# Two transformer-style blocks on one core: a sixth tile in the plain form at the head of each feed-forward network, and operand buffers moved modulo 256 bytes

## The chip, the cores and the metric

The kernel runs on one core of one Trainium2 chip. The metric is the device time of one execution in microseconds, and the time of a kernel is the median of several runs. Engines are named as in the profile: PE is TensorE (PEld is its weight load), DVE is VectorE, ACT is ScalarE, POOL is GpSimd, SP is the engine that issues the DMAs.

## The reference

An input of 512 tokens with 1024 features passes through two layers of a first block and one layer of a second block. A layer of the first block is `x += 0.5*ffn1(x)`, then a mixer of four attention variants, then `x += 0.5*ffn2(x)`, then a norm. The second block has other mixers and no feed-forward network. The change concerns the feed-forward networks alone, of which there are four (two in each layer):

```
def swiglu(h, w_gate, w_up, w_down):
    return (jax.nn.silu(h @ w_gate) * (h @ w_up)) @ w_down
```

with `h = rms_norm(x)`, 1024 features in and out, and 2816 hidden features (22 tiles of 128). All data are float32.

## The kernel before, in words

**Arithmetic.** Every float32 product is made of three matmuls in the reduced type float32r: an operand is split into a high part (an ACT copy that rounds) and a low part (a DVE subtraction), and `mm3` (line 97) adds high*high, high*low and low*high in PSUM. Tokens lie along the free dimension, so the moving operand of a matmul is an activation and the stationary operand, loaded by PEld, is a weight tile of 128x128.

**One network** (`ffn`, line 339). The 22 hidden tiles are computed one after the other by `up`, in chunks (0, 4, 8, 12, 16, 19, 22). When a chunk is done, its eight `down` steps (one for each 128 output features) are interleaved with the hidden tiles of the next chunk, two after each of them. A `down` over a chunk of four takes 12 matmuls of 512 columns, and all `down` steps of a network together take 528.

**Two forms of a hidden tile.** The first five tiles (`DIRECT = 5`) have the plain form, `direct` (line 227): for gate and up each 8 input tiles times 3 matmuls of 512 columns, 48 in all, on `xh`, `xl`, which are x times the norm's gain, split. The other 17 have a Winograd form of Strassen's product, `winograd` (line 304): gate and up are the rows of a 2x2 block product, token halves its columns, and seven products of 4 input tiles times 3 matmuls of 256 columns take the place of eight, 84 in all. Its moving operands `fh0..3`, `fl0..3` hold seven combinations of blocks of the normed input. They are made once for each network by `forms` (line 244), emitted after the first tile: per `k` two DVE scalings into temporaries `a`, `b`, four DVE subtractions into `tw`, three ACT copies into `fh` and three DVE subtractions into `fl`. `a`, `b` use the buffers `gh7`, `gl7` and `gh4`, `gl4` by turns. The weights need combinations as well, which `blocks` (line 268) makes for each tile: four sums or differences `s1` to `s4` (two on POOL, two on DVE, line 291), then seven splits (lines 298 and 299).

**Buffers of weights.** Plain tiles and `down` steps load their weights into `raw` (two buffers of 4 KB per partition in turn), and split them into `whi`, `wlo` (three buffers each). Winograd tiles load theirs into buffers of `xh`, `xl`, which are free once the plain tiles are done, but the first Winograd tile (`f == DIRECT`) loads its two halves into the two `raw` buffers (line 278) and puts `s1` to `s4` into `gh5`, `gh6`, `gl5`, `gl6`.

**Order.** A planner orders each engine's instructions by a simulated timeline; weight loads and their splits are pulled ahead by a priority offset. Each engine, and the DMA issue on SP, then runs its list in order.

**Places in SBUF.** In the compiled program of before the buffers `xh`, `xl`, `raw`, `whi`, `wlo` begin at 96 modulo 256 bytes per partition. The network's own pool (`R`, `s`, `cu`, `g..`, `f..`, `tw`) begins at 128 modulo 256, and all of its buffers are multiples of 256 bytes long. The list `PAD` (line 393) puts 0, 8, 16 and 24 floats ahead of them in the four networks. The distance from `whi`/`wlo` to `gh`, `gl`, `fh`, `fl` modulo 256 is thus 32, 64, 96 and 128 bytes in networks one to four; the distance from `whi` to `xh` is 0 in all.

**Between layers** `post_norm` (line 203) leaves a `late` function that scales the eight `x` tiles by the norm; network three (the first of layer two) calls it once after `forms` (line 381), the second block once (line 1748).

Of the kernel before, what the change touches and what calls it, by code (L numbers as in the profile page):

```python
# [12 lines left out]
F32 = mybir.dt.float32  # L13
F32R = mybir.dt.float32r
AF = mybir.ActivationFunctionType
ALU = mybir.AluOpType
# [3 lines left out]
P = 128  # L20
S = 512
D = 1024
KT = D // P
# [8 lines left out]
class Builder:  # L32
    def __init__(self, ctx, tc, A):
        self.ctx, self.tc, self.nc, self.A = ctx, tc, tc.nc, A
        self.n = 0
        self.lo_eng = tc.nc.vector
        self.late = lambda: None
        nc = self.nc
        pool = lambda name, **kw: ctx.enter_context(tc.tile_pool(name=name, bufs=1, **kw))
        self.const = pool("const")  # L40
        self.xp = pool("xp")
        self.wp = pool("wp")
        self.sm = pool("sm")
        self.ps = pool("ps", space=PSUM)
        self.ones = self.const.tile([P, P], F32, name="ones")
        nc.vector.memset(self.ones, 1.0)
        self.neghalf = self.const.tile([P, 32], F32, name="neghalf")
        nc.vector.memset(self.neghalf, -0.5)
# [154 lines left out]
    def post_norm(self, gain, bank=("t", 3)):  # L203

        nc = self.nc
        r1 = self.rstd(self.tok_sum(self.sq, bank), D)
        s2 = self.tok_sum(self.sq2, bank)
        ms = self.t(self.sm, "ms", (P, 4))
        nc.vector.tensor_tensor(out=ms, in0=s2, in1=r1, op=ALU.mult)
        nc.vector.tensor_tensor(out=ms, in0=ms, in1=r1, op=ALU.mult)  # L210
        nc.vector.tensor_scalar(out=ms, in0=ms, scalar1=1.0 / D, scalar2=EPS, op0=ALU.mult, op1=ALU.add)
        r2 = self.rsqrt(ms, (P, 4))
        r = self.t(self.sm, "r12", (P, 4))
        nc.vector.tensor_tensor(out=r, in0=r1, in1=r2, op=ALU.mult)

        def late():
            self.late = lambda: None
            R1 = self.bcast(r1, self.sm, "sqt", bank)
            for k in range(KT):
                nc.vector.scalar_tensor_tensor(out=self.x[k], in0=self.x[k], scalar=gain[:, k:k + 1], in1=R1,  # L220
                                               op0=ALU.mult, op1=ALU.mult)

        self.late = late
        return r
# [19 lines left out]
    def forms(self, gp, gain, R):  # L244


        nc = self.nc
        out = []
        lo, hi = slice(0, 256), slice(256, 512)
        flat = lambda t: t.rearrange("p e c -> p (e c)")  # L250
        sub = lambda o, x, y: nc.vector.tensor_tensor(out=o, in0=x, in1=y, op=ALU.subtract)  # L251
        for k in range(4):
            H, L = self.t(gp, f"fh{k}", (P, 7, 256), F32R), self.t(gp, f"fl{k}", (P, 7, 256), F32R)
            a, b = (self.t(gp, f"g{e}{7 - 3 * (k % 2)}") for e in "hl")
            for j, o in ((k, a), (k + 4, b)):
                nc.vector.scalar_tensor_tensor(out=o, in0=self.x[j], scalar=gain[:, j:j + 1], in1=R, op0=ALU.mult, op1=ALU.mult)
            W = self.t(gp, "tw", (P, 4, 256))
            sub(W[:, 0], a[:, hi], a[:, lo])
            sub(W[:, 1], b[:, hi], W[:, 0])
            sub(W[:, 2], b[:, hi], a[:, hi])  # L260
            sub(W[:, 3], b[:, lo], W[:, 1])
            for j, n, src in ((0, 1, a[:, lo]), (1, 2, b), (3, 4, flat(W))):
                nc.scalar.activation(out=flat(H[:, j:j + n]), in_=src, func=AF.Copy)  # L263
                sub(flat(L[:, j:j + n]), src, flat(H[:, j:j + n]).bitcast(F32))
            out.append((H, L))
        return out

    def blocks(self, gp, wgu, f):


        nc = self.nc
        with self.tc.high_priority(offset=self.ahead):
            A = []
            if f == DIRECT:
                slot = iter([(gp, f"g{t}{i}") for t in "hl" for i in (5, 6)])
                for which in range(2):
                    t = self.wp.tile([P, 1024], F32, tag="raw", name=self.name("raw"), bufs=2)
                    nc.sync.dma_start(out=t, in_=wgu[f, which])
                    A += [t[:, 0:S], t[:, S:]]
            else:  # L280
                slot = iter([(self.xp, f"x{t}{4 * (f % 2) + i}") for t in "hl" for i in range(4)])
                for which in range(2):
                    for e in range(2):
                        t = self.t(*next(slot))
                        nc.sync.dma_start(out=t, in_=wgu[f, which][:, e * S:(e + 1) * S])
                        A.append(t)
            a11, a12, a21, a22 = A
            s1, s2, s3, s4 = (self.t(*next(slot)) for _ in range(4))
            for eng, o, x, y, op in ((nc.gpsimd, s1, a21, a22, ALU.add), (nc.vector, s2, s1, a11, ALU.subtract),
                                     (nc.gpsimd, s3, a11, a21, ALU.subtract), (nc.vector, s4, a12, s2, ALU.subtract)):  # L290
                eng.tensor_tensor(out=o, in0=x, in1=y, op=op)  # L291
            out = []
            for pair in ((a11, s2), (s1, s3), (a12, s4), (a22,)):
                hi = self.wp.tile([P, 1024], F32R, tag="whi", name=self.name("whi"), bufs=3)
                lo = self.wp.tile([P, 1024], F32R, tag="wlo", name=self.name("wlo"), bufs=3)
                for e, src in enumerate(pair):
                    c = slice(e * S, (e + 1) * S)
                    nc.scalar.activation(out=hi[:, c], in_=src, func=AF.Copy)  # L298
                    nc.vector.tensor_tensor(out=lo[:, c], in0=src, in1=hi[:, c].bitcast(F32), op=ALU.subtract)  # L299
                    v = lambda t: t[:, c].rearrange("p (k m) -> p k m", k=4)  # L300
                    out.append((v(hi), v(lo)))
        return out

    def winograd(self, gp, wgu, f, F):

        nc = self.nc
        a11, s2, s1, s3, a12, s4, a22 = self.blocks(gp, wgu, f)
        pa, pb = self.bank("s", 3), self.bank("t", 3)
        lo, hi = slice(0, 256), slice(256, 512)

# [28 lines left out]
    def ffn(self, r, wgu, wd, gain, done, reorder=False):  # L339

        nc = self.nc
        with self.tc.tile_pool(name=self.name("ffn"), bufs=1, reuse_waits="tile") as gp:
            pad = next(PAD)
            if pad:
                gp.tile([P, pad], F32, name=self.name("pad"))
            R = self.bcast(r, gp, "R", ACC)
            F = None

            def up(f, i):

                u, s = self.direct(gp, wgu, f, R) if f < DIRECT else self.winograd(gp, wgu, f, F)
                nc.vector.tensor_tensor(out=u, in0=u, in1=s, op=ALU.mult)
                h = self.t(gp, f"gh{i}", dt=F32R)
                l = self.t(gp, f"gl{i}", dt=F32R)
                nc.scalar.activation(out=h, in_=u, func=AF.Copy)
                nc.vector.tensor_tensor(out=l, in0=u, in1=h.bitcast(F32), op=ALU.subtract)
                return h, l

            def down(k, f0, f1, g):

                ps = self.bank("acc", 2)
                wh, wl = self.weights(wd[k][:, f0 * P:f1 * P], (f1 - f0, P))
                for j, (h, l) in enumerate(g):
                    self.mm3(ps, wh[:, j], wl[:, j], h, l, j == 0, j == f1 - f0 - 1)
                x = self.x[k]
                if reorder and f1 == NFF:
                    t = self.t(gp, "R" if k % 2 else "xa")
                    v = lambda a: a.rearrange("p (c r) -> p r c", r=8)
                    nc.vector.scalar_tensor_tensor(out=t.rearrange("p (r c) -> p r c", r=8), in0=v(ps), scalar=0.5, in1=v(x), op0=ALU.mult, op1=ALU.add)
                    nc.scalar.activation(out=x, in_=t, func=AF.Copy)  # L370
                else:
                    nc.vector.scalar_tensor_tensor(out=x, in0=ps, scalar=0.5, in1=x, op0=ALU.mult, op1=ALU.add)  # L372

            downs = []
            for n, (f0, f1) in enumerate(zip(CHUNKS, CHUNKS[1:])):
                g = []
                for f in range(f0, f1):
                    g.append(up(f, 4 * (n % 2) + f - f0))
                    if F is None:
                        F = self.forms(gp, gain, R)  # L380
                        self.late()
                    for _ in range(-(-len(downs) // (f1 - f))):
                        downs.pop(0)()
                downs = [lambda k=k, f0=f0, f1=f1, g=g: down(k, f0, f1, g) for k in range(KT)]
# [4 lines left out]


CHUNKS = (0, 4, 8, 12, 16, 19, NFF)
DIRECT = 5
PAD = iter((0, 8, 16, 24))

POOL = 'ac'
COMB = (0, 1, 2)
# [703 lines left out]
class Mixer2(Mixer1):  # L1100
# [609 lines left out]
    def output(self, part, scratch, out=None):  # L1710
# [32 lines left out]
        if part == "x":  # L1743
            self.acc = [[self.t("oacc") for _ in range(2)] for _ in range(4)]
            for k in range(KT):
                b.x[k] = b.t(b.xp, f"x{k}")
                nc.sync.dma_start(out=b.x[k], in_=scratch[k])
            b.late()
            return
        if part != "last":  # L1750
            return first(int(part))
# [259 lines left out]
```

## Time and profile before

| what | value |
|---|---|
| median of 3 runs | 2564.03 us (2547.78 to 2564.64) |
| the profiled execution | 2554.28 us, its span 2552.4 us |
| mean granted clock of PE in it | 0.979 |
| busy PE / PEld | 2437.3 us (95%) / 2108.9 us (83%) |
| busy DVE / ACT / POOL | 1832.3 us (72%) / 1270.1 us (50%) / 718.4 us (28%) |
| read from HBM | 209.14 MB, 85 GB/s over the span |

The four networks' Winograd parts begin at 74.46, 765.17, 1124.95 and 1825.40 us of the span. Matmuls are pipelined, so a matmul's own duration in the profile (0.28 or 0.39 us) overlaps its neighbours', and the cost of one is the distance from its start to the next one's. In a table of stretches, "(x1660)" is the number of instructions that ran in the stretch, and PEclk the granted clock as a share of full speed.

### The profile page before, as it was taken

To read this page: it belongs to the slowest core of one execution; us is meant where nothing else is said; L and a number is where in the kernel's file an instruction comes from. 1 tells how busy PE (TensorE), PEld (TensorE's weight loads), DVE (VectorE), ACT (ScalarE), POOL (GpSimd) and SP (SyncE) were. 2 spreads that over 40 slices of the span, in tenths; PEclk is the share of its full clock that TensorE was granted. 3 is DMA by queue.
4 is the path that set the end of the run, shared out by engine and by line. 5 is a ranking of instruction groups with operands and counts; after the bars stand their busy time and mean duration, and the time that the engine had idled before them with its cause. 6 is when DMAs were issued, how large, how long until landed. Compare 5 with 4: busy or idle time off the path is not lost. (4 is left out here: it accounts for less than half of the span.)

```text
span 2552.4 us, 39475 instructions
## 1 busy us (share of the span) xinstructions
PE 2437.3 (95%) x14904; PEld 2108.9 (83%) x14904; DVE 1832.3 (72%) x3275; ACT 1270.1 (50%) x2422; POOL 718.4 (28%) x567
## 2 busy tenths in 40 slices
PE   8899999999999999989999999999999999899998
PEld 6899988886688999879999888767799997777867
DVE  7777776976577777797777689755877767755543
ACT  5344456676534444534444576764344445334553
POOL 1211115652212111311110447223111104452322
PEclk9899999999999999989999999999999999999999
DMA  4333233211233332323332432012333314220111
GB/s 147 110 103 106 89 119 100 90 46 37 66 107 96 105 105 73 94 92 97 103 99 67 134 102 81 20 53 75 112 100 104 104 59 148 62 76 32 41 46 56
DMA packets 113824, 220.53 MB, mean 86 GB/s; under 512 B 22160, under 2 KB 33489, under 8 KB 113633
## 3 DMA queue, kind: packets, MB, share of 16 engines
q1 hardware_dynamic: 110224, 217.67, 28.1%
q8 instruction: 117, 1.92, 0.3%
q10 hardware_dynamic: 3408, 0.33, 0.1%
q14 instruction: 75, 0.61, 0.1%
HBM read 209.14 MB, written 8.78 MB: 85 GB/s over the span
## 5 line engine op out<-in xcount | busy, mean ns | idle before, releaser
L88 ACT ACTIVATE whi<-raw 128x1024 fp32r<-128x1024 f32 (+4 forms) x343 | 263.1, 769 | 480.1 <-PE t L316 208.8
L291 POOL TENSOR_TENSOR xl<-xh,xh 128x512 f32<-128x512 f32 x128 | 190.1, 1488 | 859.9 <-DVE wlo L299 436.8
L316 PE MATMUL t<-fh,wlo 128*128 128x256 f32 x1088 | 308.5, 284 | 2.1 <-DVE wlo L299 2.1
L316 PE MATMUL t<-fh,whi 128*128 128x256 f32 x1088 | 308.0, 283 | 1.5 <-ACT fh L263 0.8
L316 PE MATMUL t<-fl,whi 128*128 128x256 f32 x1088 | 307.6, 283 | 0.0
L99 PE MATMUL acc<-gh,whi 128*128 128x512 f32 x704 | 278.1, 396 | 8.0 <-DVE x L372 4.6
L100 PE MATMUL acc<-gl,whi 128*128 128x512 f32 x704 | 279.0, 397 | 0.0
L101 PE MATMUL acc<-gh,wlo 128*128 128x512 f32 x704 | 277.3, 394 | 0.5 <-DVE wlo L89 0.5
L89 DVE TENSOR_TENSOR wlo<-raw,whi 128x512 fp32r<-128x512 f32 (+3 forms) x269 | 220.3, 819 | 51.0 <-ACT whi L88 50.1
L316 PE MATMUL s<-fh,whi 128*128 128x256 f32 x816 | 231.5, 284 | 11.3 <-ACT whi L298 6.0
L316 PE MATMUL s<-fh,wlo 128*128 128x256 f32 x816 | 231.7, 284 | 9.3 <-DVE wlo L299 9.3
L316 PE MATMUL s<-fl,whi 128*128 128x256 f32 x816 | 230.8, 283 | 1.1 <-DVE fl L251 1.1
L89 POOL TENSOR_TENSOR wlo<-raw,whi 128x1024 fp32r<-128x1024 f32 (+2 forms) x74 | 167.1, 2260 | 220.7 <-ACT whi L88 207.2
L316 PEld LDWEIGHTS t<-fh,whi 128*128 128x128 f32 x1088 | 207.5, 191 | 8.2 <-ACT whi L298 1.1
L316 PEld LDWEIGHTS t<-fl,whi 128*128 128x128 f32 x1088 | 208.0, 191 | 6.2
L316 PEld LDWEIGHTS t<-fh,wlo 128*128 128x128 f32 x1088 | 208.2, 191 | 3.0 <-DVE wlo L299 3.0
L298 ACT ACTIVATE whi<-xh 128x512 fp32r<-128x512 f32 x192 | 121.5, 633 | 178.9 <-issue 95.7
L299 DVE TENSOR_TENSOR wlo<-xh,whi 128x512 fp32r<-128x512 f32 x192 | 160.0, 833 | 33.4 <-ACT whi L298 33.0
L372 DVE SCALAR_TENSOR_TENSOR x<-acc,x 128x512 f32<-128x512 f32 x184 | 126.5, 687 | 76.1 <-PE acc L101 75.9
L298 ACT ACTIVATE whi<-xl 128x512 fp32r<-128x512 f32 x256 | 152.8, 621 | 50.1 <-PE t L316 43.5
L299 DVE TENSOR_TENSOR wlo<-xl,whi 128x512 fp32r<-128x512 f32 x256 | 169.7, 683 | 0.0
L316 PEld LDWEIGHTS s<-fh,whi 128*128 128x128 f32 x816 | 155.2, 190 | 15.6 <-ACT whi L298 6.4
(714 smaller groups left out, 6529.7 us busy)
## 6 DMA issues: line engine op xcount, KB each, us to landing
xh<-in_ffn_gu_dram SPq DMA_DIRECT2D x256, 256.0 KB, 2.6
raw<-in_ffn_d_dram SPq DMA_DIRECT2D x128, 256.0 KB, 2.7
raw<-in_ffn_gu_dram SPq DMA_DIRECT2D x48, 512.0 KB, 3.6
raw<-in_w2f_dram SPq DMA_DIRECT2D x25, 512.0 KB, 3.6
raw<-in_ffn_d_dram SPq DMA_DIRECT2D x64, 192.0 KB, 2.4
xs<-x SPq DMA_DIRECT2D x24, 256.0 KB, 4.0
raw<-in_a_dram SPq DMA_DIRECT2D x12, 512.0 KB, 3.5
x<-xs SPq DMA_DIRECT2D x24, 256.0 KB, 3.0
```

Of the source, the lines that this page charges most:

```text
L88: nc.scalar.activation(out=hi, in_=raw, func=AF.Copy)
L89: (lo_eng or self.lo_eng).tensor_tensor(out=lo, in0=raw, in1=hi.bitcast(F32), op=ALU.subtract)
L99: mm(out=out, lhsT=lh, rhs=rh, start=start, stop=False)
L100: mm(out=out, lhsT=lh, rhs=rl, start=False, stop=False)
L101: mm(out=out, lhsT=ll, rhs=rh, start=False, stop=stop)
L291: eng.tensor_tensor(out=o, in0=x, in1=y, op=op)
L298: nc.scalar.activation(out=hi[:, c], in_=src, func=AF.Copy)
L299: nc.vector.tensor_tensor(out=lo[:, c], in0=src, in1=hi[:, c].bitcast(F32), op=ALU.subtract)
L316: nc.tensor.matmul(out=out, lhsT=x[:, k], rhs=y[:, j], start=start and k == 0 and n == 0, stop=stop and k == 3 and n == 2, skip_group_chec ...
L372: nc.vector.scalar_tensor_tensor(out=x, in0=ps, scalar=0.5, in1=x, op0=ALU.mult, op1=ALU.add)
```

## The change

The diff, without the lines that only pass on an argument:

```diff
 def late():                       # in post_norm
-    self.late = lambda: None
+    self.late = lambda: lambda k: None
     R1 = self.bcast(r1, self.sm, "sqt", bank)
-    for k in range(KT):
-        nc.vector.scalar_tensor_tensor(out=self.x[k], in0=self.x[k], scalar=gain[:, k:k + 1], in1=R1,
-                                       op0=ALU.mult, op1=ALU.mult)
+    return lambda k: nc.vector.scalar_tensor_tensor(out=self.x[k], in0=self.x[k], scalar=gain[:, k:k + 1], in1=R1,
+                                                    op0=ALU.mult, op1=ALU.mult)
...
 for k in range(4):                # in forms
-    H, L = self.t(gp, f"fh{k}", (P, 7, 256), F32R), self.t(gp, f"fl{k}", (P, 7, 256), F32R)
-    a, b = (self.t(gp, f"g{e}{7 - 3 * (k % 2)}") for e in "hl")
+    H, L = (self.t(gp, f"f{e}{k}", (P, 1856), F32R)[:, 48:1840].rearrange("p (e c) -> p e c", e=7) for e in "hl")
+    a, b = (self.t(gp, f"g{e}5") for e in "hl")
...
+def quarters(self, wgu, f, slot):
+    out = []
+    for which in range(2):
+        for e in range(2):
+            t = self.t(*next(slot))
+            self.nc.sync.dma_start(out=t, in_=wgu[f, which][:, e * S:(e + 1) * S])
+            out.append(t)
+    return out
+
+def prefetch(self, gp, wgu):
+    return self.quarters(wgu, DIRECT, iter([(gp, f"g{t}{i}") for t in "hl" for i in (6, 7)]))
...
 if f == DIRECT:                   # in blocks
-    slot = iter([(gp, f"g{t}{i}") for t in "hl" for i in (5, 6)])
-    for which in range(2):
-        t = self.wp.tile([P, 1024], F32, tag="raw", name=self.name("raw"), bufs=2)
-        nc.sync.dma_start(out=t, in_=wgu[f, which])
-        A += [t[:, 0:S], t[:, S:]]
+    A = raw
+    t = [self.wp.tile([P, 1024], F32, tag="raw", name=self.name("raw"), bufs=2) for _ in range(2)]
+    s1, s2, s3, s4 = (x[:, e * S:(e + 1) * S] for x in t for e in range(2))
...
-    pad = next(PAD)               # in ffn
-    if pad:
-        gp.tile([P, pad], F32, name=self.name("pad"))
+    gp.tile([P, 56], F32, name=self.name("pad"))
+    raw = None
...
 def down(k, f0, f1, g):
+    if f0 == 0:
+        late(k)
...
-    t = self.t(gp, "R" if k % 2 else "xa")
+    t = self.t(gp, "cu")
...
     F = self.forms(gp, gain, R)
-    self.late()
+    late = self.late()
+    raw = self.prefetch(gp, wgu)
...
-DIRECT = 5
-PAD = iter((0, 8, 16, 24))
+DIRECT = 6
```

So each network computes six plain and 16 Winograd tiles. The first Winograd tile's weights are loaded in four quarters into `gh6`, `gh7`, `gl6`, `gl7`, emitted right after `forms`, and `s1` to `s4` lie in the two `raw` buffers. The temporaries of `forms` are one pair, `gh5`, `gl5`. The scaling of `x[k]` in network three goes with the first `down` of that `k`. The pool's buffers are moved by 56 floats (224 bytes) in all four networks, which puts `gh`, `gl` at 96 modulo 256, the same as `whi`, `wlo` (distance 0); `fh`, `fl` lie 48 floats further, at a distance of 192 bytes.

## Rows read from the trace of the kernel before

**Rows 1.** The page: busy time of PE and the others.
```profile
PE 2437.3 (95%) x14904; PEld 2108.9 (83%) x14904; DVE 1832.3 (72%) x3275; ACT 1270.1 (50%) x2422; POOL 718.4 (28%) x567
```
**Rows 2.** Stretches of 240 us inside networks 1 to 4: all PE (busy, count, clock, DMA).
```profile
100.00:340.00 240.00, 240.00 (x1660) 1.00 0.32 95
790.00:1030.00 240.00, 239.37 (x1676) 1.00 0.32 94
1160.00:1400.00 240.00, 240.00 (x1634) 1.00 0.32 94
1850.00:2090.00 240.00, 240.00 (x1649) 1.00 0.32 94
```
**Rows 3.** The same stretches: line 316 alone, PE then PEld.
```profile
100.00:340.00 240.00, 154.79 (x1262) 154.11 (x1263) 1.00 0.32 95
790.00:1030.00 240.00, 157.15 (x1286) 156.17 (x1285) 1.00 0.32 94
1160.00:1400.00 240.00, 156.14 (x1244) 155.04 (x1243) 1.00 0.32 94
1850.00:2090.00 240.00, 156.20 (x1259) 155.13 (x1258) 1.00 0.32 94
```
**Rows 4.** Timeline of PE, network 1: 40 plain matmuls, then 24 of `down`, first and last.
```profile
59.79 0.39 PE L101 MATMUL s<-xh,wlo 128*128 128x512 f32 x1
...
68.63 0.39 PE L101 MATMUL t<-xh,wlo 128*128 128x512 f32 x1
68.86 0.40 PE L99 MATMUL acc<-gh,whi 128*128 128x512 f32 x1
...
74.23 0.40 PE L101 MATMUL acc<-gh,wlo 128*128 128x512 f32 x1
```
**Rows 5.** Timeline of PE, network 2: 24 matmuls of `down`, first and last.
```profile
759.66 0.40 PE L99 MATMUL acc<-gh,whi 128*128 128x512 f32 x1
...
764.94 0.39 PE L101 MATMUL acc<-gh,wlo 128*128 128x512 f32 x1
```
**Rows 6.** The 30 us after the first Winograd matmul, networks 1 to 4: all PE.
```profile
74.46:104.46 30.00, 23.62 (x134) 0.77 0.20 61
765.17:795.17 30.00, 25.13 (x171) 0.94 0.27 81
1124.95:1154.95 30.00, 20.28 (x99) 0.72 0.19 55
1825.40:1855.40 30.00, 25.60 (x168) 0.89 0.27 78
```
**Rows 7.** The same stretches: line 316 alone, PE then PEld.
```profile
74.46:104.46 30.00, 18.51 (x109) 17.16 (x109) 0.77 0.20 61
765.17:795.17 30.00, 19.65 (x144) 18.69 (x144) 0.94 0.27 81
1124.95:1154.95 30.00, 14.99 (x74) 13.26 (x74) 0.72 0.19 55
1825.40:1855.40 30.00, 20.32 (x143) 19.70 (x143) 0.89 0.27 78
```
**Rows 8.** Timeline, network 1: a load of SP, and the POOL sum that waited for it.
```profile
68.12 0.38 SPq L278 DMA_DIRECT2D raw<-in_ffn_gu_dram  x1
...
74.48 1.59 POOL L291 TENSOR_TENSOR gh<-raw 128x512 f32<-128x512 f32 x1 [2.00 <-DMA raw<-in_ffn_gu_dram]
```
**Rows 9.** Timeline of PE: the longest waits of networks 2 and 3 in those stretches.
```profile
770.31 0.38 PE L316 MATMUL s<-fh,wlo 128*128 128x256 f32 x1 [3.09 <-DVE wlo L299]
...
1131.03 0.58 PE L316 MATMUL s<-fh,whi 128*128 128x256 f32 x1 [4.25 <-ACT whi L298]
```
**Rows 10.** Line 220, the 16 scalings of `x`: duration ns min/median/max, first and last start.
```profile
L220 DVE SCALAR_TENSOR_TENSOR x<-x,fin_g,sqt x16: 734/743/749, 1092.3 to 2468.1; 128x512 f32<-128x512 f32 x16
```
**Rows 11.** DMA issues: a quarter of a Winograd tile's weights, KB and us to landing.
```profile
xh<-in_ffn_gu_dram SPq DMA_DIRECT2D x256, 256.0 KB, 2.6
```
**Rows 12.** Line 263, the ACT copies of `forms`: idle before them until (us, times).
```profile
  DVE gh L256: 11.7, 6
```

More of the change, by code (lines that the diff above doesn't have):

```diff
@@ L216, in late @@
         def late():
-            self.late = lambda: None
+            self.late = lambda: lambda k: None
             R1 = self.bcast(r1, self.sm, "sqt", bank)
-            for k in range(KT):
-                nc.vector.scalar_tensor_tensor(out=self.x[k], in0=self.x[k], scalar=gain[:, k:k + 1], in1=R1,
-                                               op0=ALU.mult, op1=ALU.mult)
+            return lambda k: nc.vector.scalar_tensor_tensor(out=self.x[k], in0=self.x[k], scalar=gain[:, k:k + 1], in1=R1,
+                                                            op0=ALU.mult, op1=ALU.mult)
         self.late = late
@@ L266, in forms, with blocks @@
         return out
-    def blocks(self, gp, wgu, f):
+    def quarters(self, wgu, f, slot):
[8 more added lines that the diff above has]
+        return self.quarters(wgu, DIRECT, iter([(gp, f"g{t}{i}") for t in "hl" for i in (6, 7)]))
+    def blocks(self, wgu, f, raw):
         nc = self.nc
         with self.tc.high_priority(offset=self.ahead):
-            A = []
             if f == DIRECT:
-                slot = iter([(gp, f"g{t}{i}") for t in "hl" for i in (5, 6)])
-                for which in range(2):
-                    t = self.wp.tile([P, 1024], F32, tag="raw", name=self.name("raw"), bufs=2)
-                    nc.sync.dma_start(out=t, in_=wgu[f, which])
-                    A += [t[:, 0:S], t[:, S:]]
+                A = raw
+                t = [self.wp.tile([P, 1024], F32, tag="raw", name=self.name("raw"), bufs=2) for _ in range(2)]
+                s1, s2, s3, s4 = (x[:, e * S:(e + 1) * S] for x in t for e in range(2))
             else:
                 slot = iter([(self.xp, f"x{t}{4 * (f % 2) + i}") for t in "hl" for i in range(4)])
[L282 to L286, printed above, removed]
+                A = self.quarters(wgu, f, slot)
+                s1, s2, s3, s4 = (self.t(*next(slot)) for _ in range(4))
             a11, a12, a21, a22 = A
-            s1, s2, s3, s4 = (self.t(*next(slot)) for _ in range(4))
             for eng, o, x, y, op in ((nc.gpsimd, s1, a21, a22, ALU.add), (nc.vector, s2, s1, a11, ALU.subtract),
@@ L302, in blocks, with winograd @@
         return out
-    def winograd(self, gp, wgu, f, F):
+    def winograd(self, gp, wgu, f, F, raw):
         nc = self.nc
-        a11, s2, s1, s3, a12, s4, a22 = self.blocks(gp, wgu, f)
+        a11, s2, s1, s3, a12, s4, a22 = self.blocks(wgu, f, raw)
         pa, pb = self.bank("s", 3), self.bank("t", 3)
@@ L349, in up @@
             def up(f, i):
-                u, s = self.direct(gp, wgu, f, R) if f < DIRECT else self.winograd(gp, wgu, f, F)
+                u, s = self.direct(gp, wgu, f, R) if f < DIRECT else self.winograd(gp, wgu, f, F, raw)
                 nc.vector.tensor_tensor(out=u, in0=u, in1=s, op=ALU.mult)
@@ L1747, in output @@
                 nc.sync.dma_start(out=b.x[k], in_=scratch[k])
-            b.late()
+            late = b.late()
+            for k in range(KT):
+                late(k)
             return
```

## The prediction

> **What bounds the kernel now.** The page's first table comes first: PE is busy 95% of the span [rows 1], so time can only be won where PE waits, where its matmuls run slower than they could, or where there are fewer of them. The chain of waits, followed back from the end, gets lost in the second block and says nothing of the networks, so I went on to stretches of PE.
>
> Inside a network, past its head, PE never waits: 240.0 of 240 us busy in three networks, 239.37 in the second, at a granted clock of 1.00 [rows 2]. Yet the networks don't run alike. In equal time the second starts 1286 Winograd matmuls and the third 1244 [rows 3], with about the same number of `down` matmuls (total less Winograd: 398, 390, 390, 390 [rows 2, 3]). The only thing in the code that differs between them there is the pad.
>
> From the timelines come the spacings. Plain tiles, at distance 0: (68.63 - 59.79)/39 = 226.7 ns for a matmul of 512 columns [rows 4]. `Down` at distance 32, network one: (74.23 - 68.86)/23 = 233.5 ns [rows 4]. `Down` at distance 64, network two: (764.94 - 759.66)/23 = 229.6 ns [rows 5]. Networks three and four I cost as network one. The Winograd spacing is what is left of the busy time: (240.0 - 398 x 0.2335)/1262 = 116.5 ns in the first, (239.37 - 390 x 0.2296)/1286 = 116.5, (240.0 - 390 x 0.2335)/1244 = 119.7 and, likewise over 1259, 118.3 ns in the second to fourth [rows 2 to 5].
>
> At each network's head PE does wait. In the 30 us after the first Winograd matmul it starts 134, 171, 99 and 168 matmuls [rows 6], of which 109, 144, 74 and 143 are Winograd's [rows 7] and the other 25, 27, 25, 25 are of 512 columns. At the spacings above this is 18.5, 23.0, 14.7 and 22.8 us of work, so 11.5, 7.0, 15.3 and 7.2 us are lost, 41.0 in all. Part is idle time (30 - 23.62 = 6.4 us in network one), part the clock, granted at 0.72 to 0.94 there [rows 6].
>
> Why it waits can be followed in network one. The second half of the first Winograd tile's weights must have a `raw` buffer that the `down` weights hold before; its load is issued at 68.12 us, and the POOL sum that needs it starts at 74.48 [rows 8], when PE has already begun the tile at 74.46. The splits come later still, and PE waits for them: the longest waits of networks two and three are 3.09 us for a `wlo` and 4.25 us for a `whi` [rows 9].
>
> **The change part by part.**
>
> *Prefetch and own slots, sixth plain tile.* The four quarters no longer need `raw`, and between `forms` and the first Winograd tile stands one more plain tile: 48 x 0.2267 = 10.9 us of PE work [rows 4], in which POOL and DVE can make sums and splits and finish `forms`. That is longer than what is lost in networks one, two and four. I take a rest of 2.5 us for each network (one wait shorter than the 3.09 of [rows 9], and some time at the lower clock), 10 in all: **-31.0 us**. Bounds: nothing left, -41.0; network two's loss left in each of them, 41.0 - 4 x 7.0 = 13 won. What is late next, if anything, is the last of the four `forms`.
>
> The prefetch adds no bytes, but its four DMAs go through SP at the head, past the loads of plain tiles. A quarter takes 2.6 us to land [rows 11]. I cost it at nothing: the queue has a whole head of five plain tiles, over 50 us, to fit 10.4 us in. Without that cover it is up to 4 x 2.6 us for each network. `s1` to `s4` in `raw` hold back the weights of the next two `down` steps; these are needed after the tile's 84 x 0.1165 = 9.8 us, and a load of that size plus a split fits in that. Before, the raw weights held the same two buffers, until a later split. Nothing.
>
> *One Winograd tile less, one plain more.* 4 x 10.88 - 84 x (0.1165 + 0.1165 + 0.1197 + 0.1183) = 43.5 - 39.6 = **+4.0 us**, on the bound engine.
>
> *`gh`, `gl` at distance 0.* `Down` has the pattern of the plain tiles (512 columns, activation moving, weights stationary), which run at 226.7 ns at this distance [rows 4]. I take that: 528 x (3 x 6.8 + 2.9) ns = **-12.3 us** [rows 4, 5]. Bounds: this, and nothing won.
>
> *`fh`, `fl` at distance 192.* No row has it. The nearest by distance modulo 256 is 64 bytes on the other side of 0, network two with 116.5 ns; I take it, for want of a row that says more: 16 tiles x 84 x (0 + 0 + 3.2 + 1.8) ns = **-6.7 us**. Bounds: half of the plain spacing, 113.4 ns, gives -23.4; the worst network's 119.7 gives +10.5.
>
> A rule speaks against both placement terms. The Trainium skill ("TensorE: Matmul & The Clock Gate", Step-by-step: what each phase is for) says that weight load and moving operand have independent read ports, so that a load takes no bandwidth from the running matmul; by it, the place of one buffer against the other would not matter. The trace does not bear this out as far as the pads are the cause: the same matmul is spaced by 226.7, 229.6 and 233.5 ns at one clock.
>
> *Moved `late`, one pair `gh5`, `gl5`, `cu` for `xa`.* In network three eight scalings of 0.743 us [rows 10], 5.9 us of DVE, leave the head and go to the first `down` steps; DVE is busy 72% [rows 1], and the update of `x` that follows them holds up nobody for tens of us. Already in the stall's bounds; nothing more. With one pair, the scaling for the next `k` waits until ACT and DVE have read the last. DVE has its other work ahead of and between them, so I take nothing; the bound is a rival below. `cu` has two buffers, as `R` and `xa` together had: nothing.
>
> *Sum.* -31.0 - 12.3 - 6.7 + 4.0 = -46.0 us. Against the profiled execution's own 2554.3 us that is **2508 us**. The median of the runs shown lies 9.7 us above that execution; I keep to the execution.
>
> **The rivals.**
>
> *Placement does nothing.* The networks would differ for another reason, and only the head counts: -31 + 4 = -27, 2527 us. The rule of the Trainium skill on independent ports would give this time. Against it: the order of spacings follows the pads, and plain tiles in every network have one. Chance 0.08.
>
> *The head still waits.* The raw weights were only the last of several late things, and each network goes on losing 7.0 us: 2508 + 18 = 2526 us. For it: DVE is behind in the head, and one pair for `forms` takes freedom from the planner. Against it: 11 us more time. Chance 0.12.
>
> *The prefetch gets in the way.* Its 10.4 us of loads stand ahead of plain tiles' weights on SP, and PE waits for these instead: 4 x 10.4 = 42 us, 2550 us, no change. Against it: plain weights carry the higher priority. Chance 0.08.
>
> *Slower: the one pair of `forms`.* Three times in a network the scaling for the next `k` stands at the front of DVE's queue until the last copy is done, and behind it stand the low parts that PE needs in the plain tiles. ACT has waited 11.7 us in 6 times, 2.0 us each, at this place with two pairs [rows 12]. If each of the 12 waits costs PE as much as the longest one of [rows 9], 4.25 us, and the clock multiplies it as in network three (15.3 lost for 30 - 20.28 = 9.7 idle, 1.58), it is 12 x 4.25 x 1.58 = 81 us: 2508 + 81 = 2589 us. It turns the result to slower by 1% from 71/12 = 5.9 us lost for each wait. Against it: DVE's list is ordered with the waits known, and other work can stand ahead. Chance 0.06.
>
> **How the numbers follow.** The forecast has the rest, 0.66. The range adds up the bounds of the terms: -41.0 - 12.3 - 23.4 + 4.0 = -72.7, 2482 us; and -13 - 12.3 + 10.5 + 4.0 = -10.8, 2544 us. It holds the first two rivals; outside are the last two with 0.14 and some tails. One per cent is about what a measurement of this kernel can tell from no change. Faster by more than that needs under 2529 us on the execution's scale: nearly all of the forecast (0.62) and some over half of the first two rivals (0.12), 0.74. Slower: 0.06. Within 1%: 0.20.
>
> **What would show it.** After the change the 30 us behind the first Winograd matmul should hold some 200 matmuls or more at a clock near 1.00, and no wait over 3 us. `Down` should be spaced by 227 ns in all four networks, Winograd by one value in all four; the value is the least certain term. The plain tiles should stay free of waits; a wait there for `whi` names the prefetch, one for `wlo` names DVE's queue. I am wrong if the spacings of the four networks come out equal but at 120 ns, or if the head loses as much as before.

## The result and the profile after

| | before | after |
|---|---|---|
| median | 2556.01 us (4 runs, 2547.78 to 2564.64) | 2526.26 us (4 runs, 2519.19 to 2529.18) |
| the profiled execution | 2554.28 us | 2524.95 us |

The ratio of the changed kernel's runs to those of the kernel before is 0.9879, with a 95% interval of 0.983 to 0.9929: some 30 us faster, where 46 were forecast. The time lies inside the stated range.

The first lines of the page of the changed kernel:
```profile
span 2522.8 us, 39081 instructions
...
PE 2426.8 (96%) x14760; PEld 2102.4 (83%) x14760; DVE 1802.7 (71%) x3235; ACT 1259.5 (50%) x2394; POOL 706.3 (28%) x559
```
PE stays the bound [rows 1].

**The heads.** The 30 us after the first Winograd matmul of each network, all PE first (busy, count, clock, DMA), then the Winograd line alone, which is line 323 now:
```profile
90.45:120.45 30.00, 27.71 (x198) 1.00 0.32 89
772.14:802.14 30.00, 28.09 (x201) 1.00 0.32 92
1127.77:1157.77 30.00, 27.03 (x187) 0.94 0.28 84
1813.02:1843.02 30.00, 26.75 (x186) 0.94 0.30 88
```
```profile
90.45:120.45 30.00, 19.89 (x159) 19.40 (x159) 1.00 0.32 89
772.14:802.14 30.00, 20.26 (x162) 19.77 (x162) 1.00 0.32 92
1127.77:1157.77 30.00, 19.92 (x156) 19.22 (x155) 0.94 0.28 84
1813.02:1843.02 30.00, 20.80 (x156) 20.17 (x155) 0.94 0.30 88
```
Against 134, 171, 99 and 168 matmuls [rows 6, 7] there are now 198, 201, 187 and 186, and the clock is granted at 0.94 to 1.00 where it was 0.72 to 0.94. Worked out as in the prediction, with 117.8 and 226.8 ns, the heads lose 2.4, 2.1, 4.6 and 4.8 us: 13.9 in place of 41.0.

What is left is mostly one kind of wait, here in the timeline of PE of the changed kernel (start, duration, then in brackets the idle time before and what ended it):
```profile
98.75 0.39 PE L323 MATMUL s<-fh,whi 128*128 128x256 f32 x1 [1.75 <-DVE wu L326]
...
780.05 0.39 PE L323 MATMUL s<-fh,whi 128*128 128x256 f32 x1 [1.77 <-DVE wu L326]
...
1136.61 0.39 PE L323 MATMUL s<-fh,whi 128*128 128x256 f32 x1 [2.97 <-DVE wu L326]
...
1822.28 0.39 PE L323 MATMUL s<-fh,whi 128*128 128x256 f32 x1 [1.77 <-DVE wu L326]
```
The weights are no longer late [rows 9]: in network one the first POOL sum on them starts 13.6 us before the first Winograd matmul at 90.45 us, where it started with it before [rows 8].
```profile
76.88 2.20 POOL L298 TENSOR_TENSOR raw<-gl,gl 128x512 f32<-128x512 f32 x1 [45.99 <-DVE wlo L89]
```
PE waits for `wu`, the DVE sum that must have read the first product before PE may add `a12` to its bank. The timelines of ACT and DVE in network one show the copy that is the other input of `wu`, and `wu` itself:
```profile
93.90 0.36 ACT L331 ACTIVATE w<-s 128x256 f32<-128x256 f32 x1
...
98.28 0.41 DVE L326 TENSOR_TENSOR wu<-s,w 128x256 f32<-128x256 f32 x1
```
The input is there at 94.26 us. DVE, which is never idle in between, first works off splits of this tile, two sums for the next one and an update of `x`. The waits for `wu` are 8.3 of the 13.9 us; two waits for a `wlo`, of 0.5 and 1.5 us in networks one and four, and the lower clock in networks three and four are nearly all the rest.

**The spacings.** A stretch of 240 us inside networks one and three of the changed kernel, all PE and then line 323:
```profile
100.00:340.00 240.00, 240.00 (x1671) 1.00 0.31 92
...
1145.00:1385.00 240.00, 240.00 (x1670) 1.00 0.32 92
```
```profile
100.00:340.00 240.00, 156.93 (x1272) 156.03 (x1271) 1.00 0.31 92
...
1145.00:1385.00 240.00, 157.27 (x1272) 156.29 (x1272) 1.00 0.32 92
```
The two networks run alike now, 1272 Winograd matmuls each, where network one had 1262 and network three 1244 [rows 3]; that is still fewer than the 1286 that network two had. `Down`, 24 matmuls in network one of the changed kernel, first and last:
```profile
85.01 0.39 PE L99 MATMUL acc<-gh,whi 128*128 128x512 f32 x1
...
90.23 0.39 PE L101 MATMUL acc<-gh,wlo 128*128 128x512 f32 x1
```
(90.23 - 85.01)/23 = 227.0 ns, where it was 233.5 [rows 4] and 229.6 [rows 5].

The table gives, for every kernel, what was read in this way from its profile: the mean spacing of starts past the head, in ns, networks one to four; the loss in the four heads; the sum of the four networks (first matmul to last `down` of each); and block two, the time from the last network to the end, whose code no kernel changes.

| kernel | Winograd, ns | `down`, ns | heads, us | networks, us | block two, us |
|---|---|---|---|---|---|
| before | 116.9 116.6 119.9 118.5 | 233.2 228.9 233.7 233.5 | 40.8 | 1462.6 | 427.6 |
| after | 117.8 in all | 226.7 to 227.0 | 13.9 | 1426.0 | 434.5 |
| e1_place | 117.7 in all | 226.8 to 226.9 | 41.9 | 1451.2 | 426.0 |
| e2_head | 116.9 116.2 119.9 118.5 | 233.1 229.0 233.5 233.5 | 11.7 | 1433.7 | 424.7 |
| e3_six | 117.7 in all | 226.8 to 226.9 | 32.9 | 1446.4 | 427.4 |
| e4_pre5 | 117.7 to 117.8 | 226.7 to 226.9 | 34.5 | 1446.5 | 426.2 |
| e5_fsweep1 | 119.6 117.4 118.7 118.3 | 229.4 229.7 228.2 229.3 | 12.1 | 1434.4 | 426.8 |
| e6_fsweep2 | 118.3 119.7 118.7 118.5 | 233.8 232.7 232.8 229.3 | 12.6 | 1441.8 | 437.2 |
| e7_late | 117.8 in all | 226.8 to 227.1 | 12.3 | 1425.1 | 425.0 |
| e8_all64 | 114.5 116.7 116.7 116.7 | 229.7 229.0 229.0 229.1 | 12.2 | 1423.3 | 426.4 |
| e9_prio5 | 117.7 to 117.8 | 226.7 to 226.9 | 32.6 | 1444.8 | 426.1 |
| e10_prio6 | 117.8 in all | 226.7 to 227.1 | 12.0 | 1425.5 | 426.4 |
| e11_prio5b | 117.7 to 117.8 | 226.7 to 227.0 | 34.0 | 1444.8 | 435.7 |
| e12_mixed | 114.5 116.7 114.5 114.5 | 229.7 229.0 229.7 229.7 | 13.4 | 1417.6 | 422.2 |

### The profile page after: what moved, and what is told of

Read it like the earlier page. It is cut to its first block, busy times and chain, and to the rows that moved or that the text cites. A ratio compares the mean times of both kernels' runs of the same rounds, so it can differ in the third digit from the quotient of the medians.

```text
span 2522.8 us, 39081 instructions
## 1 busy us (share of the span) xinstructions
PE 2426.8 (96%) x14760; PEld 2102.4 (83%) x14760; DVE 1802.7 (71%) x3235; ACT 1259.5 (50%) x2394; POOL 706.3 (28%) x559
## 5 line engine op out<-in xcount | busy, mean ns | idle before, releaser
L298 POOL TENSOR_TENSOR xl<-xh,xh 128x512 f32<-128x512 f32 x120 | 175.2, 1461 | 722.2 <-DVE wlo L306 402.5
L323 PE MATMUL t<-fh,wlo 128*128 128x256 f32 x1024 | 288.8, 282 | 2.2 <-DVE wlo L306 2.0
L323 PE MATMUL t<-fh,whi 128*128 128x256 f32 x1024 | 288.6, 282 | 0.0
L323 PE MATMUL t<-fl,whi 128*128 128x256 f32 x1024 | 288.5, 282 | 0.0
L323 PE MATMUL s<-fh,whi 128*128 128x256 f32 x768 | 216.8, 282 | 8.3 <-DVE wu L326 8.3
L323 PE MATMUL s<-fh,wlo 128*128 128x256 f32 x768 | 216.5, 282 | 0.0
L323 PEld LDWEIGHTS t<-fl,whi 128*128 128x128 f32 x1024 | 192.9, 188 | 5.1
L380 DVE SCALAR_TENSOR_TENSOR x<-acc,x 128x512 f32<-128x512 f32 x184 | 126.4, 687 | 66.4 <-PE acc L101 66.0
L442 PE MATMUL acc<-whi,xh 128*128 128x256 f32 (+1 forms) x576 | 166.3, 292 | 1.9 <-DVE gate L1140 1.3
L442 PE MATMUL acc<-wlo,xh 128*128 128x256 f32 (+1 forms) x576 | 167.2, 291 | 0.4 <-DVE wlo L89 0.4
L442 PE MATMUL acc<-whi,xl 128*128 128x256 f32 (+1 forms) x576 | 166.7, 291 | 0.0
```

Source lines behind the costliest of these rows:

```text
L323: nc.tensor.matmul(out=out, lhsT=x[:, k], rhs=y[:, j], start=start and k == 0 and n == 0, stop=stop and k == 3 and n == 2, skip_group_chec ...
L442: mm = lambda l, r, st=False, sp=False: nc.tensor.matmul(out=ps[i], lhsT=l, rhs=r, start=st, stop=sp, skip_group_check=True)
```

## The experiments

My theory going in: the heads and the placement each give a part of the gain, and both can be had alone. The rivals: that placement does nothing; and, for the heads, that either the sixth plain tile or the own slots alone would do.

**e1_place: the placement alone**, on the kernel before.
```diff
-    H, L = self.t(gp, f"fh{k}", (P, 7, 256), F32R), self.t(gp, f"fl{k}", (P, 7, 256), F32R)
+    H, L = (self.t(gp, f"f{e}{k}", (P, 1856), F32R)[:, 48:1840].rearrange("p (e c) -> p e c", e=7) for e in "hl")
-    pad = next(PAD)
-    if pad:
-        gp.tile([P, pad], F32, name=self.name("pad"))
+    gp.tile([P, 56], F32, name=self.name("pad"))
-    t = self.t(gp, "R" if k % 2 else "xa")
+    t = self.t(gp, "cu")
```
Expected: 

> The placement alone: the kernel before with the pad of 56 floats in all networks and fh, fl at their offset of 48 floats; five plain tiles, raw weights and forms as before. Theory (heads and placement each give a part): down is spaced by 227 ns and Winograd by 117 to 118 ns in all four networks, some 14 us less than before in the four networks together (about 0.995 of the time), and the 30 us after the first Winograd matmul still lose 41 us in sum. Rival (placement does nothing, the spacings come from the order of the work): spacings as before, 230 to 234 ns and 116 to 120 ns by network, and no gain.

Measured: 2543.2 us, ratio 0.9971 (0.9954 to 0.9987). `Down` is at 226.8, Winograd at 117.7 ns in all four networks, these take 11.4 us less, and the heads still lose 41.9. The waits of PE in network three's head (who waited for whom, us in total, times, longest) are as before:
```profile
PE s L316 <- ACT whi L298: 4.2, 1, 4.2
PE s L316 <- ACT fh L263: 2.5, 1, 2.5
```
So buffers moved by a few dozen bytes, with no other edit that PE sees, change the spacing. The rival that placement does nothing is out.

**e2_head: the head alone**, on the changed kernel.
```diff
-    H, L = (self.t(gp, f"f{e}{k}", (P, 1856), F32R)[:, 48:1840].rearrange("p (e c) -> p e c", e=7) for e in "hl")
+    H, L = self.t(gp, f"fh{k}", (P, 7, 256), F32R), self.t(gp, f"fl{k}", (P, 7, 256), F32R)
-    gp.tile([P, 56], F32, name=self.name("pad"))
+    pad = next(PAD)                       # PAD = iter((0, 8, 16, 24))
+    if pad:
+        gp.tile([P, pad], F32, name=self.name("pad"))
```
Expected: 

> The head alone: six plain tiles, own slots, one pair for forms, late by k, with pads of 0, 8, 16 and 24 floats and no offset of fh, fl, as before. Theory: the heads lose about 15 us in all instead of 41, one plain tile more costs 4 us for four networks, so some 22 us less than before (0.991); the spacings are the ones of before, network by network (233, 230, 233, 233 ns for down). Rival (placement does nothing): the whole gain of the changed kernel, 30 us (0.988), and equal spacings in the four networks.

Measured: 2528.59 us, ratio 0.9899 (0.986 to 0.9938). Heads lose 11.7 us, the spacings are those of before to within 0.4 ns, and the networks take 28.9 us less. With e1's 11.4 that is 40.3 against 36.6 for both: the parts add up, less a few us. The ratio alone could not tell the two answers apart (the rival's 0.988 is inside the interval); the spacings do.

**e3_six: six plain tiles without own slots.**
```diff
-    A = raw
-    t = [self.wp.tile([P, 1024], F32, tag="raw", name=self.name("raw"), bufs=2) for _ in range(2)]
-    s1, s2, s3, s4 = (x[:, e * S:(e + 1) * S] for x in t for e in range(2))
+    slot = iter([(raw, f"g{t}{i}") for t in "hl" for i in (6, 7)])       # raw is gp
+    A = []
+    for which in range(2):
+        t = self.wp.tile([P, 1024], F32, tag="raw", name=self.name("raw"), bufs=2)
+        nc.sync.dma_start(out=t, in_=wgu[f, which])
+        A += [t[:, 0:S], t[:, S:]]
+    s1, s2, s3, s4 = (self.t(*next(slot)) for _ in range(4))
```
Expected: 

> The changed kernel with six plain tiles but without own slots: the first Winograd tile's weights go through the two raw buffers again, s1 to s4 into gh6, gh7, gl6, gl7. Theory (the late load of the second half is what PE waited for): the wait comes back one tile later, the heads lose 25 us or more in all, 10 us or more slower than the changed kernel. Rival (the time of one more plain tile, in which forms and DVE catch up, is what healed the heads): the heads lose about 15 us as in the changed kernel, and the time is the same.

Measured: 2535.67 us, ratio 0.9926 (0.9897 to 0.9954); the heads lose 32.9 us, networks 20.4 us more than in the changed kernel. The timelines of SP, POOL and PE of this kernel, network one (its first Winograd matmul is at 89.60 us):
```profile
80.72 0.36 SPq L292 DMA_DIRECT2D raw<-in_ffn_gu_dram  x1
...
87.06 1.29 POOL L302 TENSOR_TENSOR gh<-raw 128x512 f32<-128x512 f32 x1 [57.23 <-DMA raw<-in_ffn_gu_dram]
...
95.25 0.58 PE L327 MATMUL t<-fh,wlo 128*128 128x256 f32 x1 [3.60 <-DVE wlo L310]
```
The second half of the weights is late again: the POOL sum on it starts 2.5 us before the first Winograd matmul, against 13.6 us in the changed kernel, and PE waits for a split that follows. The sixth tile alone does not do it.

**e4_pre5: own slots with five plain tiles.**
```diff
-DIRECT = 6
+DIRECT = 5
```
Expected: 

> The changed kernel with five plain tiles: own slots and prefetch kept, placement kept. Theory (own slots heal the heads): heads lose 15 to 20 us in all, one plain tile less in each network gives 4 us back, so the time is within 5 us of the changed kernel, on either side. Rival (the sixth tile's time heals them): the heads lose 30 us or more, forms end late, and it is 12 us or more slower than the changed kernel.

Measured: 2536.91 us, ratio 0.9915 (0.9888 to 0.9942); the heads lose 34.5 us. The sum is the rival's, but not in every network: networks two and four lose 3.0 and 4.1 us, which is healed, networks one and three 12.4 and 14.9. The longest wait of PE in network one and in network three:
```profile
87.71 0.58 PE L323 MATMUL s<-fh,whi 128*128 128x256 f32 x1 [5.08 <-ACT fh L263]
...
1137.38 0.58 PE L323 MATMUL s<-fh,whi 128*128 128x256 f32 x1 [6.53 <-ACT fh L263]
```
These waits are for `forms`, not for weights. In networks one and three `forms` start 29 and 25 us after the network's first matmul and their last subtraction starts at 79 and 82 us, as it did in the kernel before (78 and 82), while the first Winograd tile of a network with five plain tiles starts at 66; in networks two and four they run from 22 to 60 us. With six plain tiles the Winograd part starts at 82 to 83 us, and the last of `forms` at 69 and 74 in networks one and three. That is what the sixth tile is for, in two networks out of four.

**e5_fsweep1, e6_fsweep2: other distances**, one run each; only pads and offset differ by network.
```diff
-    gp.tile([P, 56], F32, name=self.name("pad"))
+    pad, self.foff = next(PAD)
+    gp.tile([P, pad], F32, name=self.name("pad"))
-    [:, 48:1840]
+    [:, self.foff:self.foff + 1792]
+PAD = iter(((56, 0), (56, 16), (56, 40), (56, 56)))    # e5
+PAD = iter(((32, 36), (40, 36), (48, 40), (8, 36)))    # e6
```
Expected of e5: 

> The changed kernel with fh, fl at another distance in each network: 0, 64, 160 and 224 bytes in networks one to four; gh, gl at 0 in all. Theory (the distance modulo 256 alone sets the Winograd spacing): 64 gives the 116.4 ns that network two had before at that distance, although it is now at another pad, and the four networks differ again; 0 gives 119 to 120 ns (as the projections of the mixers, 256 columns at distance 0, spaced 119.4 ns). For 160 and 224 no number, between 114 and 120 ns. Rival (the network or the order of its work sets it): all four stay at 117.7 ns.

Expected of e6: 

> The changed kernel with fh, fl at 48, 80, 128 and 208 bytes and gh, gl at 160, 192, 224 and 64 bytes in networks one to four. Theory: 128 gives 118.5 ns and 64 bytes for down 229 ns, as before at those distances; the neighbours of 64 lie between their neighbours' values, 116.4 to 117 ns at 48 and 116.4 to 120 at 80; down at 160, 192 and 224 is slower than the 227.0 ns at distance 0, between 229 and 235 ns. Rival (the distance is not what counts): 117.7 ns and 227 ns in all four.

Measured: 2525.76 and 2542.89 us. The Winograd spacing differs by network again, so the rival (117.7 ns in all) is out: 119.6 ns at 0, 118.3 at 48, 117.4 at 64, 119.7 at 80, 118.7 at 128, 118.7 at 160, 118.5 at 208, 118.3 at 224. `Down` is worse than 227 ns at 160, 192 and 224, as expected, and 229.3 at 64. The theory that the distance alone sets it fell at two places. At 64 and 48 Winograd ran at 117.4 and 118.3, not at 116.4 to 117 ns. And `down` went to 228 to 230 ns in e5, with `gh`, `gl` at distance 0 as in the changed kernel, where it ran at 227. The timeline of PE in network two of e5 shows how: ten matmuls of `down` right behind a Winograd product, of which the first six and the last stand here.
```profile
823.33 0.40 PE L101 MATMUL acc<-gh,wlo 128*128 128x512 f32 x1
823.57 0.39 PE L99 MATMUL acc<-gh,whi 128*128 128x512 f32 x1
823.80 0.39 PE L100 MATMUL acc<-gl,whi 128*128 128x512 f32 x1
824.03 0.40 PE L101 MATMUL acc<-gh,wlo 128*128 128x512 f32 x1
824.26 0.39 PE L99 MATMUL acc<-gh,whi 128*128 128x512 f32 x1
824.49 0.40 PE L100 MATMUL acc<-gl,whi 128*128 128x512 f32 x1
...
825.41 0.39 PE L101 MATMUL acc<-gh,wlo 128*128 128x512 f32 x1
```
The mean of the nine steps from start to start is 231 ns; in the nanoseconds of the trace they begin with 241, 224, 231, 236, 228, 233 and 230 and end at 227, 227 and 226, and in longer runs of `down` they stay there. So a run behind Winograd matmuls need not start at its own spacing but can settle over several matmuls, and the place of `fh` counts for `down` too: of the places tried with `gh` at 0, only 192 for `fh` left `down` at 227 from the first matmul on. What a run takes over from the matmuls before it is not shown.

**e7_late: the scalings of network three at its head again.**
```diff
-    return lambda k: nc.vector.scalar_tensor_tensor(out=self.x[k], in0=self.x[k], scalar=gain[:, k:k + 1], in1=R1, ...)
+    for k in range(KT):
+        nc.vector.scalar_tensor_tensor(out=self.x[k], in0=self.x[k], scalar=gain[:, k:k + 1], in1=R1, ...)
+    return lambda k: None
```
Expected: 

> The changed kernel with the eight scalings of x in network three at its head again, all at once after forms. Theory (one of several loads of DVE in that head): network three's head loses 2 to 6 us more than in the changed kernel (5.1 us there), the other networks nothing, and the time of the whole is within 0.3%. Rival (they are hidden either way): no change in network three. Rival (they were what made network three the worst before): its head loses 10 us or more again.

Measured: 2515.93 us, ratio 0.9892 (0.9856 to 0.9928). Network three's head loses 4.4 us, 4.6 in the changed kernel; its networks take 1425.1 us. They are hidden either way: this part of the change is worth nothing that can be seen.

**e8_all64: the head with one pad of 8 floats**, everything at 64 bytes.
```diff
-    H, L = (self.t(gp, f"f{e}{k}", (P, 1856), F32R)[:, 48:1840].rearrange("p (e c) -> p e c", e=7) for e in "hl")
+    H, L = self.t(gp, f"fh{k}", (P, 7, 256), F32R), self.t(gp, f"fl{k}", (P, 7, 256), F32R)
-    gp.tile([P, 56], F32, name=self.name("pad"))
+    gp.tile([P, 8], F32, name=self.name("pad"))
```
Expected: 

> The changed kernel's head with the simplest placement: a pad of 8 floats in all four networks and no offset of fh, fl, so that everything is at 64 bytes, as network two was before. Theory (what the new placement won is what networks one, three and four lost against network two): the four networks run alike, Winograd at 116.4 ns and down at 229 ns, and 1344 x 116.4 + 528 x 229 ns = 277.4 us against 1344 x 117.7 + 528 x 227 = 278.0 us in the changed kernel: the same time within 3 us over four networks. Rival (distance 0 for gh with 192 for fh is better than any common one): 8 us or more slower in the four networks.

Measured: 2513.01 us, ratio 0.9862 (0.9845 to 0.988). The networks take 1423.3 us, 2.7 less than in the changed kernel. The four networks don't run alike, though I had expected it: Winograd is at 114.5 ns in network one and at 116.7 in the others. The intervals of the two ratios overlap. As far as these runs can tell, the simple pad is as good as the distances 0 and 192; the new placement won what networks one, three and four had lost by their pads.

**e9_prio5, e10_prio6, e11_prio5b: `forms` pulled ahead**, one run each.
```diff
-    F = self.forms(gp, gain, R)
+    with self.tc.high_priority(offset=60):      # e11: 150
+        F = self.forms(gp, gain, R)
-DIRECT = 6
+DIRECT = 5                                      # e10: 6
```
Expected of e9: 

> Five plain tiles with own slots, as e4_pre5, but the emission of forms pulled ahead by a priority offset of 60. Theory (in e4_pre5 networks one and three wait for the last of forms, which the order puts late): heads lose 3 to 6 us in each network, and the four networks take some 1420 to 1425 us in sum against 1426 in the changed kernel. Rival (DVE has no room for forms in five plain tiles, whatever the order): the plain tiles or the heads of networks one and three lose 10 us or more.

Expected of e10: 

> The changed kernel with forms pulled ahead by the same offset of 60, six plain tiles. Theory (the rest in the heads, a wait for wu of 1.8 to 3.0 us, comes from DVE being behind with forms): heads lose 8 us or less in all instead of 15.7. Rival (it belongs to the first Winograd tile itself, whose sums and splits come all at once): 13 us or more as before.

Expected of e11: 

> As e9_prio5 with an offset of 150, ahead of the plain tiles' own weights. Theory: forms end earlier still, but stand before the low parts of the plain tiles in DVE's list, so plain tiles lose what the heads win: sum of the four networks within 5 us of e9_prio5. Rival: heads are healed at no price, 1420 us or less.

Measured: 2533.94, 2515.52 and 2545.77 us. The offset does next to nothing: the last of `forms` in e9's networks one and three still starts 78 and 82 us after the first matmul (79 and 82 in e4), the heads of e9 and e11 lose 32.6 and 34.0 us, and those of e10 lose 12.0. PE's longest wait in network three of e9 is the one of e4:
```profile
1137.05 0.58 PE L323 MATMUL s<-fh,whi 128*128 128x256 f32 x1 [6.89 <-ACT fh L263]
```
So priority is no lever here. The loss that e9's rival names came, and e11 is within 5 us of e9 in the networks, but with `forms` where they were this doesn't tell whether DVE has room for them in five tiles under another order. In e10 the wait for `wu` stays, and the 12.0 us are neither the 8 of the theory nor the 13 of its rival. The 12 us between e11 and e9 are mostly block two's.

**e12_mixed: everything at 64, six plain tiles in networks one and three, five in two and four.**
```diff
+    self.D = next(DIR)                          # DIR = iter((6, 5, 6, 5)), in place of DIRECT
```
Expected: 

> As e8_all64 (everything at 64 bytes, own slots), with six plain tiles in networks one and three and five in networks two and four, where forms end 59 us after the network's first matmul and the first Winograd tile starts 66 us after it. Theory (how many plain tiles a network needs is set by when its forms end): networks two and four lose 3 to 5 us in their heads, as in e4_pre5, and save 1 us each, so the four networks take some 1421 us in sum (1423.3 in e8_all64), at a ratio of 0.986 to the kernel before. Rival (own slots need the sixth tile everywhere): networks two and four lose 7 us or more each.

Measured: 2513.56 us, ratio 0.9836 (0.9792 to 0.9879). Heads of networks two and four lose 2.6 and 3.4 us: five plain tiles do there once the weights have own slots, and the rival is out. The networks take 1417.6 us, the least of all and 5.7 less than in e8. As much as that, 2.2 ns x (1344 + 1428) = 6.1 us, comes from Winograd being at 114.5 ns in networks three and four, so the 2 us expected of the two plain tiles can't be told apart from it. It has the lowest ratio of all kernels, with an interval that overlaps those of e8 and of the changed kernel.

## Why the prediction was right, and where its terms were off

The side, the range and the mechanisms held, the size less well. The time alone would not have shown the mechanisms: 2526 us lies 18 us above the forecast and on the times of two rivals, placement that does nothing (2527) and a head that still waits (2526). What tells them apart are the stages, and e1 and e2. By the prediction's own steps:

*The heads, -31.0 forecast.* 41.0 - 13.9 = 27.1 us won. The mechanism was right: the late load is gone. By e3 the own slots are needed for it; by e4 and e12 the sixth plain tile is needed in networks one and three, where `forms` end late, and not in two and four. "What is late next" I put down as the last of `forms`; it is that with five plain tiles in networks one and three (e4), while in the changed kernel it is `wu`. With the lower clock behind it the rest is 3.5 us for each network instead of the 2.5 I took. One reading beside this term was wrong: the 10.9 us of a plain tile are less than the 11.5 that network one lost.

*One plain tile more, +4.0.* 4 x 48 x 0.2268 - 84 x (0.1169 + 0.1166 + 0.1199 + 0.1185) = +3.9 us.

*`gh`, `gl` at distance 0, -12.3.* 528 x (6.4 + 2.1 + 6.9 + 6.7) ns = -11.7 us. The plain tiles' row was the right one to take.

*`fh`, `fl` at 192, -6.7.* This step failed by size. 16 x 84 x (-0.9 - 1.2 + 2.1 + 0.7) ns = 0.7 ns x 1344 = -0.9 us: networks three and four won, one and two lost. That 192 would be like 64 for being as far from 0 had no row behind it; it gives 117.8 ns, not 116.5. The bounds (113.4 to 119.7) held.

*The sum* by measured terms is -27.1 + 3.9 - 11.7 - 0.9 = -35.8; the networks themselves went from 1462.6 to 1426.0, -36.6. The span went down by 29.5 only, because block two took 6.9 us more in the changed kernel's profile. That is not the change: with the same code there, block two took from 422.2 to 437.2 us in the twelve other changed profiles, nine of them between 424.7 and 427.4. It goes with the granted clock there: 0.930 to 0.932 in the three profiles over 434 us, 0.948 to 0.965 in the eleven others. Each of those three has a stretch of 23.9 us at 0.50, the lower of the clock's two levels (1.2 GHz); in the others no such stretch in block two is longer than 13.7 us. Here it is in the changed kernel, and below the same place in e7_late, whose block two took 425.0 us (all PE: busy, count, clock, DMA):
```profile
2438.10:2461.90 23.80, 23.80 (x85) 0.50 0.06 17
...
2437.90:2461.70 23.80, 23.80 (x141) 0.93 0.05 17
```
PE was busy throughout in both, and in the 10 us before; the same 85 matmuls take 23.8 us in the first and 15.2 us in the second. Why the clock stayed low in the one is not shown. The prediction had no term for this scatter. So the 16 us missing of the 46 are about 4 in the heads, 6 in `fh`, and 7 in block two of this execution.

*The rivals.* That placement does nothing is refuted by e1: 226.8 against 233.2 ns for `down` in network one by a move of the buffers alone. The Trainium skill ("TensorE: Matmul & The Clock Gate", Step-by-step: what each phase is for) has it that loading the next weights takes no read bandwidth from the running matmul. The prediction read from this that the place would not matter, and in these traces it does; whether it is the weight load that takes the time, no run shows. The head that still waits, at 28 us in all, would have come nearer without the sixth tile (34.5) or without own slots (32.9). The prefetch got in nobody's way, and the single pair of `forms` held up no plain tile: the Winograd parts start 82.4 to 82.8 us after the networks' first matmuls, against 66.1 to 66.4 before, 16.4 us more, and one plain tile and two `down` steps more are 48 x 0.2268 + 24 x 0.2268 = 16.3 us.

*What would show it.* I had asked for some 200 matmuls behind the first Winograd matmul (186 to 201 came), no wait over 3 us (2.97), `down` at 227 ns in all four networks (it is), and one Winograd value in all four (117.8). A clock near 1.00 came in networks one and two only; in three and four it was 0.94.

## What to carry to other kernels

Where PE is busy nearly all the time, read the distance between the starts of successive matmuls by stage: the same instruction at one clock ran from 226.8 to 233.8 ns here, and the buffers' places were the cause, so try two or three pads, measure the whole loop and not one kind of matmul, and keep the simplest. When a first use stalls, follow every input of it; here the weights and the moving operands were late together, and curing one alone left most of the loss. And time a change by the stages it can touch: the unchanged rest moved by up to 15 us between executions, with the granted clock, and that is half the gain.

## What the runs showed of the hardware that was not expected

The Winograd matmuls have more than one rhythm at one clock, and at a given distance can be in either. In e12, with the same pad in all networks, 60 matmuls in a row in network one and 60 in network two, first and last of each in the timeline of PE:
```profile
199.74 0.28 PE L323 MATMUL s<-fh,whi 128*128 128x256 f32 x1
...
206.43 0.28 PE L323 MATMUL s<-fh,wlo 128*128 128x256 f32 x1
```
```profile
894.08 0.28 PE L323 MATMUL s<-fh,whi 128*128 128x256 f32 x1
...
901.03 0.28 PE L323 MATMUL s<-fh,wlo 128*128 128x256 f32 x1
```
(206.43 - 199.74)/59 = 113.4 ns and (901.03 - 894.08)/59 = 117.8 ns. The first is half of a 512-column matmul's 226.8. By their means of 114.5 and 116.7 ns, some three quarters of the Winograd matmuls are in the fast rhythm in network one of e8 and e12 and a quarter in network two; in the changed kernel, at 117.8, almost none. What puts PE in the one or the other, beyond the distances and the matmuls just before, stays open. A placement that holds the fast rhythm throughout would be worth some 4.4 ns x 5376 = 24 us against the changed kernel, an estimate from these two rows; none of those tried does.

Why the place counts at all is open too. No run moved `whi`, `wlo`, so the distance to them can't be told from the place of the moving buffers by itself, and nothing here shows what PE loses its time to.
